# Value products placed among the next unit's scores, and the modulation's steps, PSUM banks and tiles of a fused Fourier/attention layer divided anew

## The chip, the cores and the metric

The kernel runs on one core of a Trainium2 chip. The core has five engines with instruction streams of their own, which meet only through semaphores: TensorE (PE, matmuls into PSUM banks; its weight loads are listed as PEld), VectorE (DVE), ScalarE (ACT), GpSimd (POOL), and SyncE (SP), which here issues nearly all DMA transfers. The metric is the device time of one execution in microseconds, as the median of several runs.

## The reference

One step of a diffusion layer on 1024 latent and 128 context tokens, width 1024, all in fp32. The six modulation vectors come from the conditioning vector and `w_ada`; the first two are needed at the start, the other four only behind the attention. Condensed:

```python
def latent_layer(x, mod, k_ctx, v_ctx, cos, sin, g1, g2, w_in, sink, w_fo, w_ao, w_out, w_ff1, w_ff2):
    sh1, sc1, ga1, sh2, sc2, ga2 = mod          # silu(c) @ w_ada + b_ada, split in six
    h = rmsnorm(x, g1) * (1 + sc1) + sh1
    u_f, q, k, v, g = split_projection(h, w_in) # 512, 1024, 256, 256, 2048 columns
    q, k = apply_rope(q, cos, sin), apply_rope(k, cos, sin)   # 16 heads, 4 key/value heads
    attn_o = latent_attention(q, k, v, k_ctx, v_ctx, sink)    # window of +-128, context keys, sink
    x = x + ga1 * merge_branches(u_f, attn_o, g, w_fo, w_ao, w_out)
    h = rmsnorm(x, g2) * (1 + sc2) + sh2
    return x + ga2 * channel_mixer(h, w_ff1, w_ff2)

def merge_branches(u_f, attn_o, g, w_fo, w_ao, w_out):
    g_f, g_a = split(sigmoid(g))
    m = g_f * (fourier_mix(u_f) @ w_fo) + g_a * (attn_o @ w_ao)   # fourier_mix: real part of a 2-D DFT
    return m @ w_out
```

The context tokens go through the same layer and see only context keys.

## The kernel before

Every fp32 product is made of reduced-precision parts. An operand is split into a high part (a cast, on ScalarE: names in `hi` or `h`) and the rest (a subtraction, on VectorE: names in `lo` or `l`, line 140), and a product is three matmuls, high x high, high x low, low x high (lines 193, 194, 195). Where only one operand is split it is two.

The stages follow each other: normalization and the U projection (to 100 us of the profile), the Fourier mixer in four groups of channels (100 to 176), keys and values and the queries of the first head group (176 to 256), the attention (256 to 716), the Fourier output product `f_unit` (lines 907, 909, 923) around the attention's end (to 740), the merge with `w_ao`, `w_out`, and the two feed-forward products, from about 950 to the end.

**The attention** has 36 units: four groups of four heads, by nine tiles of 128 query tokens. A unit reads 1 to 4 key blocks of 128 (`KWIN`). For each of its heads `score_head` makes the scores in a PSUM bank `s` (lines 752, 753: query by `kth`, `ktl`), VectorE adds the mask and takes the maximum (754), ScalarE takes the exponential (764) and, for each pair of heads, GpSimd divides by the sum (776). `out_t` then transposes a key block of the probabilities into a bank `ptp` (786) and splits it into `ph` (789) and `pl` (140); `out_v` multiplies these with the values into the one bank `o` (801, 802), which behind the last block is copied out by ScalarE (`ot`, 810) and VectorE (`at`, 811). In a round the scores of one unit are followed by the transposes and products of the unit before. The order of TensorE is written out by hand (`manual_schedule`) for the first 34 units; `fill_to` spreads among them single steps of three matmuls of 24-matmul pieces: the queries of the next groups and the gate projections. Other engines' orders are set by the scheduler.

Key blocks are transposed by `put_k` (832), in banks of the same name `ptp`, four blocks at a time, and split into `kth` (834) and `ktl`.

**The modulation** for the later four vectors is 160 small steps (`mod_blocks`): sixteen blocks of ten, eight multiplications and two reductions. A multiplication loads 128 KB into `mraw` (299), multiplies on ScalarE (two instructions, 303; the first of a block into `macc`, the others into the single tile `mprod`) and adds on GpSimd (305). A reduction transposes `macc` into a tile of the name `mraw` too and sums it on VectorE (321, 322); `mod_fold` adds up across partitions on TensorE (268). `mod_step(n)` does the next n steps. Of the 160, 100 are done in the attention, 3 a unit as `MOD_A` says, 20 in the merge stage, where the multiplication is one VectorE instruction (312), and 40 in the feed-forward stage. The Fourier output units use the tile `macc` as their buffer.

Of the kernel before, what the change touches and what calls it, by code (L numbers as in the profile page):

```python
# [18 lines left out]
P = 128  # L19
# [23 lines left out]
KWIN = {0: (0, 3), 1: (0, 4), 2: (1, 4), 3: (3, 4), 4: (4, 4), 5: (6, 4), 6: (7, 4), 7: (8, 3), 8: (11, 1)}  # L43
FILL_F = 2
FILL_0 = 3
MOD_A = (2, 1)
MOD_2 = 2
MOD_B = 60
MOD_LATE = 40
NF = 4  # L50
NF2 = 2
# [5 lines left out]
def backbone_kernel(  # L57
# [185 lines left out]
    MB = 256  # L243

    mview_z = [None, 0]
    MRB = [2, 1]
    split_mul = [True]

    def macc_tile():
# [4 lines left out]
    def mraw_tile():  # L254
        if mview_z[0] is not None:
            mview_z[1] ^= 1
            return mview_z[0][:, 512 + MB * mview_z[1] : 512 + MB + MB * mview_z[1]]
        return zpool[0].tile([P, MB], F32, tag="mraw", name=nm("mraw"), bufs=MRB[0])

    fold = []  # L260

# [24 lines left out]
    def mod_blocks():  # L286
        for blk in range(2 * D // MB, 6 * D // MB):
            st = {}
            for k in range(10):

                def step(blk=blk, k=k, st=st):
                    if k == 5:
                        mod_fold()
                    if k == 0:
                        st["a"] = macc_tile()
                    acc = st["a"]
                    if k < 8:
                        wa = mraw_tile()
                        nc.sync.dma_start(wa, w_ada[k * P : (k + 1) * P, blk * MB : (blk + 1) * MB])
                        if split_mul[0]:  # L300
                            pr_ = acc if k == 0 else zpool[0].tile([P, 2, MB], F32, tag="mprod", name=nm("mprod"), bufs=1)
                            for tok in range(2):
                                nc.scalar.activation(pr_[:, tok, :], wa, AF.Copy, scale=siluc[:, tok, k : k + 1])  # L303
                            if k:
                                nc.gpsimd.tensor_tensor(acc, acc, pr_, ALU.add)  # L305
                            return
                        for tok in range(2):
                            sc_ = siluc[:, tok, k : k + 1]
                            if k == 0:
                                nc.vector.tensor_scalar(acc[:, tok, :], wa, sc_, None, ALU.mult)  # L310
                            else:
                                nc.vector.scalar_tensor_tensor(
                                    acc[:, tok, :], wa, sc_, acc[:, tok, :], ALU.mult, ALU.add
                                )
                        return
                    if k == 8:
                        st["r"] = const.tile([P, 2, MB // 32], F32, tag="red", name=nm("red"), bufs=2)
                    red = st["r"]
                    tok = k - 8
                    tr = mraw_tile()  # L320
                    nc.vector.transpose(tr, acc[:, tok, :])
                    nc.vector.tensor_reduce(
                        red[:, tok, :], tr.rearrange("p (c j) -> p c j", j=32), mybir.AxisListType.X, ALU.add
                    )
                    if k == 9:
                        fold.append((blk, red))

                yield step
# [8 lines left out]
    with ExitStack() as sf:  # L337
# [175 lines left out]
        for gi in range(4):  # L513
# [64 lines left out]
            if e == 1:  # L578
                for i, (lat, o) in enumerate(((bx, 0), (by, 130))):
# [2 lines left out]
                    nc.scalar.copy(f[:, 512:FC], bc[:, o : o + 130])  # L582
                    nc.sync.dma_start(f_d[2 * i + gi // 2], f)
            filler(FILL_F, anchor)

    with ExitStack() as s1x:
        p1 = s1x.enter_context(tc.tile_pool(name="p1", bufs=1))
# [72 lines left out]
        with ExitStack() as skv:  # L660
# [58 lines left out]
            put_kd(kc_, 9)  # L719
            tok_proj_round(ROUNDS[0], OFF_KV, bankk, evac_kv)  # L720
            tok_proj_round(ROUNDS[1], OFF_KV, bankk, evac_kv)
            for piece in q_pieces(0):
                for _ in piece:
                    pass

        pq = s1x.enter_context(tc.tile_pool(name="pq", bufs=1))
        q1 = s1x.enter_context(tc.tile_pool(name="q1", bufs=1, space=PSUM))

# [7 lines left out]
        def score_head(u, h):  # L736
# [10 lines left out]
                u["mx"] = mx  # L747
                nc.gpsimd.tensor_copy(pt[:, :, n : n + 1], nsink[:, h0 : h0 + 2].unsqueeze(2))
            pt, mx = u["pts"][-1], u["mx"]
            sp = q1.tile([P, 512], F32, tag="s", name=nm("s"), bufs=3)  # L750
            qs = qT[:, h, (i % 3) * P : (i % 3 + 1) * P]
            nc.tensor.matmul(sp[:, :n], qs, kth[:, k0 * P : k0 * P + n], start=True, stop=False)
            nc.tensor.matmul(sp[:, :n], qs, ktl[:, k0 * P : k0 * P + n], start=False, stop=True)  # L753
# [27 lines left out]
                    mod_step(min(MOD_A[pr], len(msteps) - MOD_B))  # L781

        def out_t(u, b):
            pst = q1.tile([P, 512], F32, tag="ptp", name=nm("ptp"), bufs=2)
            for h in range(4):
                nc.tensor.transpose(pst[:, h * P : (h + 1) * P], u["pts"][h // 2][:, h % 2, b * P : (b + 1) * P], ident)  # L786
            ph = p1.tile([P, 512], F32R, tag="ph", name=nm("ph"), bufs=3)
            pl = p1.tile([P, 512], F32R, tag="pl", name=nm("pl"), bufs=3)
            nc.scalar.copy(ph, pst)  # L789
            sub(nc.vector, pl, pst, ph)  # L790
            u["p"][b] = ph, pl

        def out_v(u, b):
# [8 lines left out]
            nc.tensor.matmul(po, vst, pl, start=False, stop=(b == nb - 1))  # L802
            if b < nb - 1:
                return
            ot = p1.tile([P, 2, P], F32, tag="ot", name=nm("ot"), bufs=2)
            at = p1.tile([P, 2, P], F32, tag="at", name=nm("at"), bufs=2)
            pv = po.rearrange("p (r e t) -> p e r t", r=2, e=2)
            for e in range(2):
                top, bot = slice(64 * e, 64 * e + 64), slice(64 - 64 * e, 128 - 64 * e)
# [16 lines left out]
            return kd, vg  # L826

        def put_k(kd, q):
            pk = q1.tile([P, 512], F32, tag="ptp", name=nm("ptp"), bufs=2)
            for b in range(4):  # L830
                kb = {"c": 9, "x": 8}.get(KT_ORDER[q * 4 + b], KT_ORDER[q * 4 + b])
                nc.tensor.transpose(pk[:, b * P : (b + 1) * P], kd[:, kb].rearrange("p a d -> p (a d)"), ident)
# [102 lines left out]

        units = [(g, i) for g in range(NG) for i in range(NTT)]
        kv = {0: load_kv(0, kd0)}
        for q in range(3):
            put_k(kv[0][0], q)

# [41 lines left out]

        NMAN = len(units) - 2
        wsum = sum(weight(s) for s in range(NMAN))
        qts = {(0, 0): load_qt(0, 0)}

        def begin(s):
            g, i = units[s]
            if i % 3 == 0 and s + 3 < len(units):
                g1, i1 = units[s + 3]  # L990
                assert g1 in qdone, (s, g1)
                qts[g1, i1 // 3] = load_qt(g1, i1 // 3)
            return {"g": g, "i": i, "q": qts[g, i // 3], "v": kv[g][1], "pts": [], "p": {}}

        def next_keys(g, i):
# [7 lines left out]
                if i == 7:  # L1003
                    put_k(kv[g + 1][0], 1)

        man = ExitStack()
        man.enter_context(tc.manual_schedule(engines={mybir.EngineType.PE}))
        base, pending = 0.0, None
        for s in range(NMAN):
            u = begin(s)  # L1010
            nb = KWIN[pending["i"]][1] if pending else 0
            spots = 4 + (2 * nb + 1 if pending else 0)
            share = NSUB * weight(s) / wsum
            seen = [0]

            def gap():
                seen[0] += 1
                fill_to(base + share * seen[0] / spots)

            for h in range(4):  # L1020
                score_head(u, h)
                gap()
            for b in range(nb):
                out_t(pending, b)
                gap()
                if b:
                    out_v(pending, b - 1)
                gap()
            if nb:
                gap()  # L1030
                out_v(pending, nb - 1)
            base += share
            fill_to(base)
            next_keys(*units[s])
            pending = u
        fill_to(NSUB)
# [3 lines left out]
        for s in range(NMAN, len(units)):  # L1040
            u = begin(s)
            for h in range(4):
                score_head(u, h)
            nb = KWIN[pending["i"]][1]
            for b in range(nb):
                out_t(pending, b)
# [1033 lines left out]
```

## Time and profile before

| | us |
|---|---|
| median of three runs (lowest, highest) | 1684.17 (1682.91, 1687.2) |
| the profiled execution | 1687.13 |
| its span between first and last instruction | 1685.2 |
| TensorE busy | 1624.9 |
| VectorE, ScalarE, GpSimd busy | 1137.1, 897.0, 268.2 |
| mean granted clock of TensorE | 0.993 |

The profile is one execution. A row of a timeline reads: start, duration, engine, line, operation, written tile<-read tiles, shape, count, and in brackets how long the engine had been idle before and what ended that. Where a row stands for several instructions its duration covers them all. Waits are sums of such idle times by the line that waited and the one that ended it. A row of the view by windows gives the stretch, its length, the busy time of PE, PEld, DVE, ACT and POOL with the number of instructions, the granted clock, the DMA engines' share and GB/s. Rows of groups give busy time and mean duration in ns, then the idle time before and what ended it.

### The profile page before, as it was taken

How to read it: one execution, taken by the hardware profiler on the slowest of the kernel's cores; microseconds unless marked ns; L12 is line 12 of the kernel's file. 1: busy time of each engine (PE TensorE's matmuls, PEld its weight loads, DVE VectorE, ACT ScalarE, POOL GpSimd, SP SyncE). 2: the span in 40 equal slices, each digit the busy share in tenths (PEclk: the TensorE clock that was granted, in tenths of full speed). 3: DMA queues.
4: the chain of work that ended last, by engine and by line, in shares of the span. 5: the costliest groups of instructions: out<-in, count | busy, mean ns of one | idle time of the engine just before them, and what ended most of it. 6: DMA issues, size and time to landing. Idle time of an engine off the chain costs nothing.

```text
span 1685.2 us, 24900 instructions
## 1 busy us (share of the span) xinstructions
PE 1624.9 (96%) x8421; PEld 1422.9 (84%) x8421; DVE 1137.1 (67%) x2179; ACT 897.0 (53%) x1743; POOL 268.2 (16%) x368
## 2 busy tenths in 40 slices
PE   6999999999989999999999999999999999999998
PEld 5889888888879889889987788888888888888887
DVE  7663258757657766769657876777776498776764
ACT  7743226767666676655346665444444363444542
POOL 1010014444444444300001500000000200000000
PEclk9999999999999999999999999999999999999999
DMA  8441495435553442389565434445546996666751
GB/s 292 137 148 69 142 218 162 130 111 138 113 123 96 141 114 76 113 267 290 171 206 176 163 113 161 151 158 168 172 143 160 310 389 194 193 194 193 251 162 63
DMA packets 221135, 285.40 MB, mean 169 GB/s; under 512 B 30968, under 2 KB 148664, under 8 KB 220880
## 3 DMA queue, kind: packets, MB, share of 16 engines
q1 hardware_dynamic: 212752, 273.85, 51.6%
q0 software_dynamic: 8256, 9.96, 2.6%
q8 instruction: 66, 1.08, 0.3%
q14 instruction: 61, 0.50, 0.1%
HBM read 205.87 MB, written 77.88 MB: 168 GB/s over the span
## 4 chain that ended last, share of the span: by engine, by line
PE 64%; DVE 9%; DMA 4%; ACT 4%; issue 3%; POOL 2%; SPq 0%; DVEq 0%; ACTq 0%; POOLq 0%
PE x L1806 6%; PE x L1807 6%; PE x L1805 6%; PE x L1409 6%; PE x L1411 6%; PE x L1410 6%; PE mm L193 3%; PE mm L195 3%; PE mm L194 3%; PE ptp L786 2%; DVE pt L754 2%; PE o L802 2%; PE x L194 1%; PE x L195 1%; PE x L193 1%
## 5 line engine op out<-in xcount | busy, mean ns | idle before, releaser
L140 DVE TENSOR_TENSOR wlo<-wraw,whi 128x1024 fp32r<-128x1024 f32 x109 | 138.4, 1272 | 94.7 <-ACT whi L145 94.7
L145 ACT CAST whi<-wraw 128x1024 fp32r<-128x1024 f32 x107 | 111.7, 1049 | 94.6 <-DMA wraw<-in_w_in_dram 18.3
L194 PE MATMUL mm<-BR,whi 128*128 128x384 f32 x408 | 138.5, 339 | 0.0
L1806 PE MATMUL x<-BR 128*128 128x512 f32 (+1 forms) x348 | 132.9, 382 | 0.0
L1807 PE MATMUL x<-BR 128*128 128x512 f32 (+1 forms) x348 | 132.3, 382 | 0.0
L1805 PE MATMUL x<-BR 128*128 128x512 f32 (+1 forms) x348 | 131.4, 382 | 0.0
L193 PE MATMUL mm<-BR,whi 128*128 128x384 f32 x360 | 129.5, 360 | 0.3 <-DVE mods L272 0.3
L140 DVE TENSOR_TENSOR pl<-ptp,ph 128x512 fp32r<-128x512 f32 x124 | 84.7, 687 | 65.2 <-ACT ph L789 64.7
L776 POOL TENSOR_SCALAR pt<-pt,mx 128x512 f32<-128x512 f32 (+2 forms) x144 | 94.7, 670 | 206.3 <-DVE mx L774 204.2
L195 PE MATMUL mm<-BR,wlo 128*128 128x384 f32 x360 | 122.9, 341 | 0.0
L764 ACT ACTIVATE pt<-pt,mx 128x513 f32<-128x513 f32 (+2 forms) x144 | 95.2, 662 | 21.0 <-DVE mx L754 16.5
L1778 ACT CAST BR<-aa 128x512 fp32r<-128x512 f32 x80 | 49.7, 621 | 104.1 <-issue 46.2
L754 DVE CUSTOM_DVE_ANT_0 pt<-s,mask,nsink 128x512 f32<-128x512 f32 (+2 forms) x144 | 94.5, 670 | 14.3 <-PE s L753 11.6
L305 POOL TENSOR_TENSOR macc<-macc,mprod 128x512 f32<-128x512 f32 x70 | 92.4, 1320 | 14.9 <-ACT mprod L303 14.5
L789 ACT CAST ph<-ptp 128x512 fp32r<-128x512 f32 x124 | 70.9, 578 | 41.7 <-PE ptp L786 37.2
L1409 PE MATMUL x<-BR,whi 128*128 128x512 f32 (+2 forms) x204 | 79.6, 390 | 4.1 <-ACT ZR L1433 2.8
L194 PEld LDWEIGHTS mm<-BR,whi 128*128 128x128 f32 x408 | 78.1, 191 | 5.6
L1411 PE MATMUL x<-BR,wlo 128*128 128x512 f32 (+2 forms) x204 | 78.2, 383 | 0.0
L1410 PE MATMUL x<-BR,whi 128*128 128x512 f32 (+2 forms) x204 | 78.0, 382 | 0.0
L193 PE MATMUL mm<-BT,whi 128*128 128x384 f32 x216 | 77.1, 357 | 0.0
L140 DVE TENSOR_TENSOR BR<-aa,BR 128x512 fp32r<-128x512 f32 x80 | 55.2, 690 | 32.4 <-ACT BR L1778 31.5
L786 PE MATMUL ptp<-ident,pt 128*128 128x128 f32 x496 | 75.1, 274 | 1.8 <-POOL pt L776 0.9
(450 smaller groups left out, 4736.3 us busy)
## 6 DMA issues: line engine op xcount, KB each, us to landing
aa<-hr_d SPq DMA_DIRECT2D x108, 256.0 KB
ab<-in_w_ff_dram SPq DMA_DIRECT2D x108, 256.0 KB
hr_d<-ZR SPq DMA_DIRECT2D x104, 256.0 KB
wraw<-in_w_in_dram SPq DMA_DIRECT2D x41, 512.0 KB
wraw<-in_w_ff_dram SPq DMA_DIRECT2D x34, 512.0 KB
mraw<-in_w_ada_dram SPq DMA_DIRECT2D x96, 128.0 KB
wraw<-in_w_out_dram SPq DMA_DIRECT2D x24, 512.0 KB
z_d<-z SPq DMA_DIRECT2D x48, 192.0 KB
```

The lines of the kernel that those rows point to most:

```text
L140: eng.tensor_tensor(dst, raw, hi.bitcast(F32), ALU.subtract)
L145: nc.scalar.copy(hi, raw)
L193: nc.tensor.matmul(out, ah, bh, start=start, stop=False)
L194: nc.tensor.matmul(out, ah, bl, start=False, stop=False)
L195: return nc.tensor.matmul(out, al, bh, start=False, stop=stop).ins
L754: nc.vector.tensor_tensor_reduce(out=pt[:, e, :n], in0=sp[:, :n], in1=mask[:, m0 : m0 + n], scale=-0.125, scalar=nsink[:, h0 + e : h0 + e ...
L1409: nc.tensor.matmul(po, wh, xh, start=(k == 0 and not cont), stop=False, skip_group_check=cont)
L1410: nc.tensor.matmul(po, wh, xl, start=False, stop=False, skip_group_check=cont)
L1411: nc.tensor.matmul(po, wl, xh, start=False, stop=(k == 3), skip_group_check=cont)
L1805: nc.tensor.matmul(ps, xh, bh, start=start, stop=False, skip_group_check=cont)
L1806: nc.tensor.matmul(ps, xh, bl, start=False, stop=False, skip_group_check=cont)
L1807: nc.tensor.matmul(ps, xl, bh, start=False, stop=stop, skip_group_check=cont)
```

## The change

It has six parts.

1. *Value products.* In the hand-written order, product 0 of the unit before follows two fill gaps behind the transposes of block 2 (behind the last where there are fewer than three). Products 1 to 3 are kept in a list and issued one behind each of the next unit's scores. The last two units, which are not ordered by hand, take what is left in the list between their scores.
2. *PSUM banks.* `s` has two banks for three, `ptp` three for two.
3. *Tiles.* `mraw` has three buffers for two, and the transposed result a tile of its own, `mtr`; `ot` and `at` have one buffer for two.
4. *Modulation.* Ten steps behind each of the four Fourier groups, two a unit for three, eight behind the last unit, none in the merge stage, 40 late as before.
5. *First queries and keys.* The six pieces of the first group's queries and the three `put_k` of its keys stand in the hand-written order, one behind the other.
6. *Query loads.* `begin` loads the first tiles too.

```diff
-MOD_A = (2, 1)
+MOD_A = (1, 1)
-MOD_B = 60
+MOD_B = 40
+MOD_F = 10
...
-    MRB = [2, 1]
+    MRB = [3, 1]
...
+    def mtr_tile():
+        if mview_z[0] is not None:
+            return mraw_tile()
+        return zpool[0].tile([P, MB], F32, tag="mtr", name=nm("mtr"), bufs=1)
...
-                    tr = mraw_tile()
+                    tr = mtr_tile()
...
             filler(FILL_F, anchor)
+            mod_step(MOD_F)
...
             tok_proj_round(ROUNDS[1], OFF_KV, bankk, evac_kv)
-            for piece in q_pieces(0):
-                for _ in piece:
-                    pass
...
-            sp = q1.tile([P, 512], F32, tag="s", name=nm("s"), bufs=3)
+            sp = q1.tile([P, 512], F32, tag="s", name=nm("s"), bufs=2)
...
-            pst = q1.tile([P, 512], F32, tag="ptp", name=nm("ptp"), bufs=2)
+            pst = q1.tile([P, 512], F32, tag="ptp", name=nm("ptp"), bufs=3)
...
-            ot = p1.tile([P, 2, P], F32, tag="ot", name=nm("ot"), bufs=2)
-            at = p1.tile([P, 2, P], F32, tag="at", name=nm("at"), bufs=2)
+            ot = p1.tile([P, 2, P], F32, tag="ot", name=nm("ot"), bufs=1)
+            at = p1.tile([P, 2, P], F32, tag="at", name=nm("at"), bufs=1)
...
         kv = {0: load_kv(0, kd0)}
+        man = ExitStack()
+        man.enter_context(tc.manual_schedule(engines={mybir.EngineType.PE}))
+        for piece in q_pieces(0):
+            for _ in piece:
+                pass
         for q in range(3):
             put_k(kv[0][0], q)
...
+        def unit_order(s, u, prev, late):
+            nb = KWIN[prev["i"]][1] if prev else 0
+            out = []
+            for h in range(4):
+                out += [lambda h=h: score_head(u, h), None]
+                if late:
+                    out += [lambda v=late.pop(0): out_v(*v), None]
+            for b in range(nb):
+                out += [lambda b=b: out_t(prev, b), None]
+                if b == 2:
+                    out += [None, lambda: out_v(prev, 0), None]
+            if 0 < nb < 3:
+                out += [None, lambda: out_v(prev, 0), None]
+            late += [(prev, b) for b in range(1, nb)]
+            return out
...
-            for h in range(4):
-                score_head(u, h)
-                gap()
-            for b in range(nb):
-                out_t(pending, b)
-                gap()
-                if b:
-                    out_v(pending, b - 1)
-                gap()
-            if nb:
-                gap()
-                out_v(pending, nb - 1)
+            for f in order:
+                if f is None:
+                    seen += 1
+                    fill_to(base + share * seen / spots)
+                else:
+                    f()
...
             for h in range(4):
                 score_head(u, h)
+                if late:
+                    out_v(*late.pop(0))
```

In the order of the changed kernel lines are numbered three to twelve higher: 752 is 755, 786 is 789, 801 is 804, 810 is 813, 832 is 835, 303 is 309, 911 is 914.

TensorE in the middle of a unit, before: the transposes of block 1 of the unit before (`ptp<-ident,pt`), a filling step, the product of block 0 (`o<-ph`, `o<-pl`), a filling step, the transposes of block 2.

```order
L786 MATMUL ptp_5693<-ident,pt_5441 128x128 x2
L786 MATMUL ptp_5693<-ident,pt_5475 128x128 x2
L193 MATMUL mm_5622<-BT,whi_5344 128x384
L194 MATMUL mm_5622<-BR,whi_5344 128x384
L195 MATMUL mm_5622<-BT,wlo_5345 128x384
L801 MATMUL o_5719<-ph_5680,vg_4058 128x512
L802 MATMUL o_5719<-pl_5681,vg_4058 128x512
L193 MATMUL mm_5722<-BR,whi_5242 128x384
L194 MATMUL mm_5722<-BR,whi_5242 128x384
L195 MATMUL mm_5722<-BR,wlo_5243 128x384
L786 MATMUL ptp_5726<-ident,pt_5441 128x128 x2
L786 MATMUL ptp_5726<-ident,pt_5475 128x128 x2
```

The changed kernel in the middle of a unit, first among the scores: a score, a filling step, the product of block 2 of the unit before (its third into the bank `o_5677`), a filling step, the next score.

```order
L755 MATMUL s_5719<-kth,qT_5133 128x512
L756 MATMUL s_5719<-ktl,qT_5133 128x512
L194 MATMUL mm_5710<-BR,whi_5449 128x384
L195 MATMUL mm_5710<-BR,whi_5449 128x384
L196 MATMUL mm_5710<-BR,wlo_5450 128x384
L804 MATMUL o_5677<-ph_5667,vg_4206 128x512
L805 MATMUL o_5677<-pl_5668,vg_4206 128x512
L194 MATMUL mm_5710<-BR,whi_5449 128x384
L195 MATMUL mm_5710<-BR,whi_5449 128x384
L196 MATMUL mm_5710<-BR,wlo_5450 128x384
L755 MATMUL s_5744<-kth,qT_5133 128x512
L756 MATMUL s_5744<-ktl,qT_5133 128x512
```

And behind the transposes of block 2, where the product of block 0 is the first into a new `o`:

```order
L789 MATMUL ptp_5830<-ident,pt_5541 128x128 x2
L789 MATMUL ptp_5830<-ident,pt_5579 128x128 x2
L194 MATMUL mm_5814<-BR,whi_5360 128x384
L195 MATMUL mm_5814<-BR,whi_5360 128x384
L196 MATMUL mm_5814<-BR,wlo_5361 128x384
L194 MATMUL mm_5814<-BR,whi_5360 128x384
L195 MATMUL mm_5814<-BR,whi_5360 128x384
L196 MATMUL mm_5814<-BR,wlo_5361 128x384
L804 MATMUL o_5845<-ph_5810,vg_4206 128x512
L805 MATMUL o_5845<-pl_5811,vg_4206 128x512
```

Between the transposes of block 1 and the product of block 0 lay one filling step; now the transposes of block 2 and two steps more lie behind it, and the other products stand in the next round.

TensorE where the queries of the first group end, before. The key transposes (`ptp<-ident,kd`) of the first eight blocks stand between two pieces (`mm_2124` and `mm_2163` are two pieces' banks); the scores begin 49 rows later.

```order
L193 MATMUL mm_2124<-BT,whi_2052 128x384
L194 MATMUL mm_2124<-BR,whi_2052 128x384
L195 MATMUL mm_2124<-BT,wlo_2053 128x384
L832 MATMUL ptp_2243<-ident,kd_1621 128x128
L832 MATMUL ptp_2250<-ident,kd_1621 128x128 x4
L193 MATMUL mm_2163<-BR,whi_2017 128x384
L194 MATMUL mm_2163<-BR,whi_2017 128x384
L195 MATMUL mm_2163<-BR,wlo_2018 128x384
```

In the changed kernel: the last piece, all twelve transposes, the first score.

```order
L194 MATMUL mm_2440<-BT,whi_2300 128x384
L195 MATMUL mm_2440<-BT,whi_2300 128x384
L196 MATMUL mm_2440<-BT,wlo_2301 128x384
L835 MATMUL ptp_2479<-ident,kd_1855 128x128 x4
L835 MATMUL ptp_2486<-ident,kd_1855 128x128 x4
L835 MATMUL ptp_2493<-ident,kd_1855 128x128 x4
L755 MATMUL s_2513<-kth,qT_2500 128x384
L756 MATMUL s_2513<-ktl,qT_2500 128x384
```

All three sets now stand between the last query piece and the first score, which reads the first set's `kth` and `ktl`.

ScalarE at the end of the attention, before: copies of the last units (`ot<-o`), the last split (`ph`), and between them the copies of the Fourier output units (`macc<-mm`, `kd<-mm`, `z<-mm`).

```order
L810 COPY ot_7501<-o_7465 64x256
L911 COPY macc_7794<-mm_7779 128x512
L789 CAST ph_7894<-ptp_7889 128x512
L810 COPY ot_7710<-o_7685 64x256
L914 COPY kd_7795<-mm_7780 128x1
L810 COPY ot_7710<-o_7685 64x256
L925 COPY z_7816<-mm_7802 128x130
L911 COPY macc_7863<-mm_7848 128x512
L810 COPY ot_7901<-o_7898 64x256
```

In the changed kernel the copies of the last two units alternate with the multiplications of the last modulation steps (`mprod<-mraw`), and the copy `macc<-mm` of a Fourier output unit follows behind the last of these.

```order
L813 COPY ot_7783<-o_7758 64x256
L309 ACTIVATE mprod_7907<-mraw_7905,siluc 128x256 x2
L813 COPY ot_7783<-o_7758 64x256
L309 ACTIVATE mprod_7921<-mraw_7919,siluc 128x256 x2
L813 COPY ot_8025<-o_8022 64x256
L309 ACTIVATE mprod_7927<-mraw_7925,siluc 128x256 x2
L813 COPY ot_8025<-o_8022 64x256
L309 ACTIVATE mprod_7933<-mraw_7931,siluc 128x256 x2
L146 CAST whi_8139<-wraw_8134 128x1024
L914 COPY macc_7826<-mm_7811 128x512
```

The multiplications are new in this place, and the copies for the Fourier output units moved behind them.

More of the change, by code (lines that the diff above doesn't have):

```diff
@@ L828, in put_k @@
         def put_k(kd, q):
-            pk = q1.tile([P, 512], F32, tag="ptp", name=nm("ptp"), bufs=2)
+            pk = q1.tile([P, 512], F32, tag="ptp", name=nm("ptp"), bufs=3)
             for b in range(4):
@@ L984, in backbone_kernel @@
         wsum = sum(weight(s) for s in range(NMAN))
-        qts = {(0, 0): load_qt(0, 0)}
+        qts = {}
         def begin(s):
             g, i = units[s]
[L989 to L992, printed above, removed]
+            for g1, i1 in units[s : s + 4 : 3] if i % 3 == 0 else ():
+                if (g1, i1 // 3) not in qts:
+                    assert g1 in qdone, (s, g1)
+                    qts[g1, i1 // 3] = load_qt(g1, i1 // 3)
             return {"g": g, "i": i, "q": qts[g, i // 3], "v": kv[g][1], "pts": [], "p": {}}
@@ L1004, in next_keys @@
                     put_k(kv[g + 1][0], 1)
-        man = ExitStack()
-        man.enter_context(tc.manual_schedule(engines={mybir.EngineType.PE}))
-        base, pending = 0.0, None
+        def unit_order(s, u, prev, late):
[13 more added lines that the diff above has]
+            return out
+        base, pending, late = 0.0, None, []
         for s in range(NMAN):
             u = begin(s)
-            nb = KWIN[pending["i"]][1] if pending else 0
-            spots = 4 + (2 * nb + 1 if pending else 0)
+            order = unit_order(s, u, pending, late)
             share = NSUB * weight(s) / wsum
[L1014 to L1018, printed above, removed]
-            for h in range(4):
-                score_head(u, h)
-                gap()
-            for b in range(nb):
-                out_t(pending, b)
-                gap()
-                if b:
-                    out_v(pending, b - 1)
-                gap()
-            if nb:
-                gap()
-                out_v(pending, nb - 1)
+            spots, seen = order.count(None), 0
+            for f in order:
[4 more added lines that the diff above has]
+                    f()
             base += share
-            fill_to(base)
             next_keys(*units[s])
```

## Prediction

> **What bounds the kernel now.** I read the page first, then TensorE's waits for the stretch of the attention, then single waits in the timeline.
>
> ```profile
> PE 1624.9 (96%) x8421; PEld 1422.9 (84%) x8421; DVE 1137.1 (67%) x2179; ACT 897.0 (53%) x1743; POOL 268.2 (16%) x368
> ```
>
> TensorE is busy for 1624.9 of 1685.2 us and the change takes no matmul away, so all that can be won is its idle time, about 60 us, and time at a reduced clock. The waits of TensorE from 250 to 716 us (what was waited for: us, times, longest):
>
> ```profile
> PE o L802 <- DVE pl L140: 8.8, 19, 1.9
> PE o L801 <- ACT ph L789: 8.6, 8, 5.0
> ```
>
> These are value products that wait for their probabilities' high part (`ph`, ScalarE) or low part (`pl`, VectorE): 17.4 us. The largest of them:
>
> ```profile
> 470.80 0.80 PE L801 MATMUL o<-ph,vg 128*128 128x512 f32 x1 [5.01 <-ACT ph L789]
> 466.78 0.91 ACT L303 ACTIVATE macc<-mraw,siluc 128x256 f32<-128x256 f32 x2 [4.74 <-DMA mraw<-in_w_ada_dram]
> 460.02 8.02 SPq L299 DMA_DIRECT2D mraw<-in_w_ada_dram x3
> 563.92 0.51 PE L802 MATMUL o<-pl,vg 128*128 128x512 f32 x1 [1.89 <-DVE pl L140]
> 431.53 0.51 PE L802 MATMUL o<-pl,vg 128*128 128x512 f32 x1 [1.08 <-DVE pl L140]
> ```
>
> The first is a product of block 0; `ph` was late because ScalarE stood for 4.74 us at a modulation step whose load SyncE could not issue (8.02 us in the queue): the transposed result held one of the two `mraw` buffers. The second is of block 2, the third of block 3. Each such wait followed to its block in this way: blocks 1 to 3 have 5.3 us, block 0 has 12.4, of which 5.0 are the one above and 7.4 lie in 13 units, none over 1.2. The first and the last of these:
>
> ```profile
> 270.22 0.49 PE L801 MATMUL o<-ph,vg 128*128 128x512 f32 x1 [0.92 <-ACT ph L789]
> 629.02 0.50 PE L802 MATMUL o<-pl,vg 128*128 128x512 f32 x1 [0.41 <-DVE pl L140]
> ```
>
> Two of these waits also cost clock:
>
> ```profile
> 468.40:476.00 7.60, 5.20 (x16) 4.39 (x17) 2.23 (x5) 3.79 (x10) 2.29 (x4) 0.55 0.26 78
> 564.00:570.00 6.00, 6.00 (x23) 5.48 (x24) 3.51 (x8) 1.55 (x4) 0.00 (x0) 0.72 0.66 210
> 564.43 0.35 PE L194 MATMUL mm<-BR,whi 128*128 128x384 f32 x1
> 564.61 0.50 PE L195 MATMUL mm<-BR,wlo 128*128 128x384 f32 x1
> 564.90 0.52 PE L193 MATMUL mm<-BR,whi 128*128 128x384 f32 x1
> 565.22 0.52 PE L194 MATMUL mm<-BR,whi 128*128 128x384 f32 x1
> ```
>
> The column after POOL is the granted clock, 0.55 and 0.72. Starts of matmuls of 384 columns lie 0.18 us apart before 564.6 and 0.32 after, so a microsecond of work at the low clock loses 0.45. The 5.2 busy us of the first row ran so, and 3.4 us of the second (6 us at a mean of 0.72): 2.3 + 1.5 = 3.8 us.
>
> **The change, part by part.** Blocks 1 to 3 now stand between the next unit's scores. From their transposes to them lie at least 18 more filling matmuls (18 x 0.18 = 3.2 us) with transposes and scores beside; none of their waits was over 1.9 us, so **-5.3**. Block 0 has twelve filling matmuls and two sets of transposes behind its own, where it had twelve and one: 0.4 us more. In the 13 units this leaves 2.9 of 7.4, so **-4.4**. The 5.0 goes if modulation never stalls ScalarE so long: a third `mraw` buffer, an own tile for the transposes, two steps a unit for three; **-5.0**, with **-3.8** of clock. Bounds for the four: -5.3 and -21.2. What comes late next is the single `o` bank: product 0 of a unit must wait for both copies behind the last product of the unit before, which now lies some 5.4 us earlier in TensorE's work. Two score banks for three are no wait by the same working: nine filling matmuls, two products and a score lie between a bank's uses.
>
> The 20 steps of the merge stage go, and with them one wait:
>
> ```profile
> PE mm L268 <- DVE red L322: 1.3, 1, 1.3
> ```
>
> **-1.3**; the 20 steps themselves were VectorE's work beside a busy TensorE.
>
> The start of the attention: the query pieces of group 0 and the key transposes (L832) are now in written order.
>
> ```profile
> 236.51 0.41 PE L832 MATMUL ptp<-ident,kd 128*128 128x128 f32 x2 [2.80 <-ACT rb L708]
> 255.69 1.05 ACT L145 CAST whi<-wraw 128x1024 fp32r<-128x1024 f32 x1 [3.11 <-PE mm L194]
> 256.65 0.58 ACT L834 CAST kth<-ptp 128x512 fp32r<-128x512 f32 x1
> 257.81 1.22 DVE L140 TENSOR_TENSOR wlo<-wraw,whi 128x1024 fp32r<-128x1024 f32 x1
> 258.95 0.55 DVE L636 TENSOR_TENSOR qt<-qt,qt 128x384 f32<-128x384 f32 x1
> 259.42 0.68 DVE L140 TENSOR_TENSOR ktl<-ptp,kth 128x512 fp32r<-128x512 f32 x1
> ```
>
> Before, the transposes of the first four key blocks went between pieces and their casts were done when the scores began. Now they follow the last piece, and right behind them come scores that need `kth` and `ktl`. From the piece's end: weight cast 1.05 on ScalarE, its low part 1.22 on VectorE, L636 0.55 and `ktl` 0.68 make 3.5, with some 0.4 between; TensorE, through with the transposes, has `kth` for the first score at 1.7 and asks for `ktl` at 1.9. **+2.0**, and 0.4 more for `kth` and for the third score's bank, which VectorE frees behind the same queue. The 2.80 wait stays but for 0.45, since the third piece needs rotary steps that VectorE ends then. By the rows a wait of 1.89 brought the low clock, ones of 1.08 and 1.31 did not, so I add one period, **+1.5**. Sum +3.5, bounds -2.8 (the wait of 236.5 gone) and +5.
>
> The Trainium skill ("TensorE: Matmul & The Clock Gate", section "What's actually happening") has the clock halve only after an idle window of about 3.4 us. By that the 2.0 us would cost no clock and this term be 1.5 less; the 1.89 us wait above, with its low clock from 564.6 on, speaks against it.
>
> The U projection and the Fourier stage take 40 steps: 32 multiplications with an addition each, and eight reductions.
>
> ```profile
> 83.26 3.04 ACT L344 COPY u<-x 128x512 f32<-128x512 f32 x6 [3.46 <-PE x L233]
> 81.46 0.34 SPq L664 DMA_DIRECT2D rope<-in_rope_dram  x1
> L303 ACT ACTIVATE mprod<-mraw,siluc 128x256 f32<-128x256 f32 x138 | 62.9, 503 | 20.9 <-POOL macc L305 20.3 <-DMA mraw<-in_w_ada_dram 0.5
> L305 POOL TENSOR_TENSOR macc<-macc,mprod 128x512 f32<-128x512 f32 x70 | 92.4, 1320 | 14.9 <-ACT mprod L303 14.5
> 100.00:126.00 26.00, 25.31 (x146) 24.31 (x145) 19.67 (x28) 12.16 (x20) 6.86 (x7) 1.00 0.51 155
> 126.00:150.00 24.00, 24.00 (x143) 22.39 (x142) 8.21 (x24) 8.53 (x17) 1.49 (x2) 1.00 0.23 84
> 143.07 0.59 ACT L581 COPY f<-x 128x512 f32<-128x512 f32 x1 [3.50 <-PE x L195]
> ```
>
> ScalarE's first step stands ahead of the six copies that free U's banks, and its load can be issued only when the tiles of the stage before go, at 81.5: about **+1.5** for TensorE (0 to 3). From there to 176 us the 32 steps are 32 x (2 x 0.50 + 1.32) = 74 us of a chain over ScalarE and GpSimd, in 93 us where ScalarE is a third busy and waits 2 to 3.5 us for TensorE in each group. So most hides there; for copies that stand behind a step that waits for its addition I take **+3** (0 to 12).
>
> The end of the attention: eight steps stand behind the last unit's. Before, there were none.
>
> ```profile
> 707.94 1.74 POOL L776 TENSOR_SCALAR pt<-pt,mx 128x128 f32<-128x128 f32 x2 [1.90 <-DVE mx L774]
> 711.78 0.63 PE L786 MATMUL ptp<-ident,pt 128*128 128x128 f32 x4 [0.86 <-DVE pl L140]
> 718.82 0.74 PE L907 MATMUL mm<-BR,whi 128*128 128x512 f32 x2 [0.44 <-ACT z L925]
> 721.40 0.50 PE L801 MATMUL o<-ph,vg 128*128 128x512 f32 x1 [0.91 <-DVE at L811]
> 726.56 0.70 PE L907 MATMUL x<-BR,whi 128*128 128x512 f32 x2 [1.11 <-DVE at L811]
> ```
>
> From GpSimd's last normalization (709.7) to the first product in the next stage's banks (726.6) TensorE waited 3.3 us. In the new order of ScalarE the six last multiplications alternate with the copies of the last two units (L810), and each waits for the addition before it, as `mprod` is one buffer. The copy that frees the last bank stands behind the fifth: 1.3 + 4 x 2.3 + 1.0 + 0.7 = 12.2 us after the normalization. `macc` is needed by the Fourier output units too, so these can't fill in until the chain is through; TensorE has about 3 us of work. Idle 9.2 for 3.3: **+6**, a clock period **+1.5**, and **+1** as the merge's loads start nearer to their use. Sum +8.5, bounds 0 (the chain is done before) and +14 (loads late by 5).
>
> **Sum**: -5.3 - 4.4 - 5.0 - 3.8 - 1.3 = -19.8, and 3.5 + 1.5 + 3 + 8.5 = +16.5: -3.3 us. The profiled execution took 1687.1 around its span of 1685.2; the median of the three runs is 1684.2. The same difference from the median gives **1681**.
>
> **Rivals.** *The added work hides* (28%): the chain at the end finds its steps done early because GpSimd is idle for most of the tail, and the Fourier stage swallows its steps; then only the 3.5 and 1.5 are left, with 1 us for the rest: -13.8, 1670. For it: the idle times of ScalarE above. Against it: one `mprod` buffer, 20.3 us of waiting for the addition in the row above.
>
> *GpSimd's additions hold VectorE up in the Fourier stage* (17%), slower:
>
> ```profile
> 101.40 1.79 DVE L518 TENSOR_TENSOR st<-u 128x512 f32<-128x512 f32 x1
> 109.27 0.69 DVE L518 TENSOR_TENSOR st<-u 128x512 f32<-128x512 f32 x1
> 101.33 1.31 POOL L519 TENSOR_TENSOR e<-u 128x512 f32<-128x512 f32 x1 [75.94 <-ACT u L344]
> ```
>
> One instruction took 1.79 us beside a GpSimd addition and 0.69 without. The page of the Trainium skill "GPSIMD Engine Reference", section "1. Specifications", has GpSimd share VectorE's interface to the memory, with contention for instructions of two inputs there; the trace agrees by these rows. Four such instructions a group, 1.1 late each, are 4.4 against some 3 us of slack: 1.4 x 4 groups; with one held-up ScalarE copy of 1.3 a group and 1 us at the first, 12 us for my 3: 1690. It decides from where additions lie beside the group's preparation rather than its products. Against it: VectorE is a third busy from 126 on.
>
> *Block 0 doesn't gain* (13%): its small waits stay at 7.4, for the copies of `o` now lie just ahead: +4.4, 1685.5.
>
> **How the numbers follow.** The forecast has 42%. Of it about 9 points lie below 1679.1, the rest within 0.3% (5 us, about what a measurement of this kernel can tell from no change). Faster: 27 points of the first rival and these 9, 0.36. Slower: 14 of the second, 5 of the third and 3 of the forecast, 0.22. Within: 0.42. The forecast's own range is 1675 to 1689; for 8 in 10 it reaches to both outer rivals and past them by a part of their bounds, 1667 to 1695.
>
> **What would show it.** Right: the waits of `o` for `ph` and `pl` fall from 17.4 to about 3 us and the clock stays full from 260 to 690; a wait of about 2 us at the first score for `ktl`; one of about 9 us at the first product in the `x` banks for `at` near the end of the attention; in the Fourier stage single waits for `pqh` or `sth` of 1 us. Wrong: no wait at the end of the attention (first rival), or additions beside lengthened VectorE instructions and over 8 us of waits before 176 (second).

## The result and the profile after

The changed kernel takes **1695.51 us** (median of 4 runs, 1692.07 to 1696.1) against 1683.54 us (4 runs, 1682.18 to 1687.2): a ratio of 1.0063, with a 95% interval of 1.0042 to 1.0085. It is slower, where 1681 and no clear difference had been forecast, and lies just above the range of 1667 to 1695. The profiled execution took 1695.82 us for 1687.13, its span is 1694.0 us for 1685.2. That is 8.8 us where the medians are 12.0 apart: the profiled execution of the kernel before is near the slowest of its runs. In the changed kernel's rows the lines of the shared helpers are numbered one higher than before (140 is 141, 193 to 195 are 194 to 196).

First TensorE's waits of the changed kernel in the stretch of the units, 260 to 690 us (what was waited for: us, times, longest):

```profile
PE s L756 <- DVE ktl L141: 5.0, 1, 5.0
PE o L804 <- DVE at L814: 2.9, 1, 2.9
PE o L805 <- DVE pl L141: 1.6, 5, 0.8
PE o L804 <- ACT ph L792: 1.2, 2, 0.8
```

The waits for `ph` and `pl` fell from 17.4 to 2.8 us, as forecast; what had not been there is the wait for `ktl` (forecast as 2) and the one for the copies out of `o`. Then 690 to 760 us, where the attention ends:

```profile
PE o L804 <- DVE at L814: 7.6, 2, 4.1
PE x L910 <- DVE at L814: 3.8, 1, 3.8
PE x L194 <- ACT ER L1128: 3.1, 1, 3.1
PE x L910 <- ACT fy L914: 1.6, 1, 1.6
PE mm L910 <- DVE mods L278: 1.2, 1, 1.2
PE x L912 <- ACT fo L917: 1.0, 1, 1.0
```

and the same stretch by windows (length, busy PE, PEld, DVE, ACT, POOL, granted clock, DMA share, GB/s), the changed kernel first, then the kernel before from the same place in its work:

```profile
690.00:760.00 70.00, 51.04 (x233) 42.68 (x233) 35.65 (x70) 29.76 (x71) 15.48 (x17) 0.78 0.53 166
706.00:776.00 70.00, 65.66 (x377) 60.22 (x376) 51.02 (x98) 38.78 (x81) 4.82 (x9) 1.00 0.81 253
```

In 70 us TensorE idles 19 us for 4, and the clock is 0.78 for 1.00. The rest is read from four marks, before and after: the first product of U, the last product of the Fourier stage, the first score, and the first product of the stage behind the merge.

```profile
35.71 0.40 PE L231 MATMUL x<-whi,BR 128*128 128x512 f32 x1
172.72 0.28 PE L575 MATMUL x<-pxl,dhi 128*128 128x130 f32 x1
256.03 0.42 PE L752 MATMUL s<-kth,qT 128*128 128x384 f32 x1
843.43 0.48 PE L1240 MATMUL x<-whi,BR 128*128 128x512 f32 x1
```

```profile
33.55 0.40 PE L232 MATMUL x<-whi,BR 128*128 128x512 f32 x1
178.73 0.28 PE L581 MATMUL x<-pxl,dhi 128*128 128x130 f32 x1
260.08 0.44 PE L755 MATMUL s<-kth,qT 128*128 128x384 f32 x1
851.95 0.39 PE L1251 MATMUL x<-whi,BR 128*128 128x512 f32 x1
```

The first product of U starts 2.16 us earlier, which the change doesn't account for: over the profiles of all runs it starts between 33.2 and 36.1 with no order in it. From there to the last Fourier product 137.0 us became 145.2, **+8.2**. From that to the first score it is 2.0 us less: the wait of 2.80 us at 236.5 with its low clock is gone, one of 1.9 us at 241.7 with full clock has come. From the first score to behind the merge 587.4 became 591.9, **+4.5**, where -19.8 of gains and +3.9 and +8.5 of costs had been forecast. From there to the end the two differ by 0.3 us.

### The profile page after: what moved, and what is told of

Same layout as the page of the kernel before. It is cut to its first block, busy times and chain, and to the rows that moved or that the text cites. A ratio compares the mean times of both kernels' runs of the same rounds, so it can differ in the third digit from the quotient of the medians.

```text
span 1694.0 us, 24957 instructions
## 1 busy us (share of the span) xinstructions
PE 1624.9 (96%) x8421; PEld 1430.3 (84%) x8421; DVE 1134.8 (67%) x2147; ACT 912.3 (54%) x1775; POOL 290.4 (17%) x382
## 3 DMA queue, kind: packets, MB, share of 16 engines
q8 instruction: 66, 1.08, 0.3%
## 4 chain that ended last, share of the span: by engine, by line
PE 49%; DVE 2%; issue 2%; ACT 1%; DMA 1%; POOL 0%; SPq 0%; POOLq 0%; ACTq 0%; DVEq 0%
PE x L1817 6%; PE x L1816 6%; PE x L1818 6%; PE x L1420 6%; PE x L1422 6%; PE x L1421 6%; PE x L196 2%; PE x L194 2%; PE x L195 2%; PE mm L1467 1%; PE mm L1466 1%; PE mm L1465 1%; PE mm L1817 1%; PE mm L1816 1%; PE mm L1818 1%
## 5 line engine op out<-in xcount | busy, mean ns | idle before, releaser
L311 POOL TENSOR_TENSOR macc<-macc,mprod 128x512 f32<-128x512 f32 x84 | 113.5, 1352 | 108.3 <-ACT mprod L309 97.3
L309 ACT ACTIVATE mprod<-mraw,siluc 128x256 f32<-128x256 f32 x168 | 76.8, 505 | 32.1 <-POOL macc L311 31.8
```

## The experiments

Each was timed beside the kernel before on the same chip, in at least four runs.

**e1**, no steps behind the last unit.

```diff
-MOD_B = 40
+MOD_B = 50
```

> The changed kernel with MOD_B 50: no modulation step behind the last unit, ten in the merge stage again. Theory (the chain of eight steps at the end costs about 11 us of waits for at and some 9 us of low clock up to 756 us): 12 to 20 us less than the changed kernel, 1676 to 1683, and the three waits of 4.10, 3.52 and 3.82 us gone. Rival (TensorE has run ahead and waits there in any case, for one bank o and single ot and at): the waits stay over 8 us in sum, 1690 to 1696.

1669.29 us; 0.9910 of before (0.9892 to 0.9927). That is 26 us less than the changed kernel, more than the theory asked for. The stretch of 690 to 760 us in this kernel:

```profile
690.00:760.00 70.00, 66.71 (x384) 62.17 (x383) 53.92 (x107) 39.48 (x84) 3.83 (x8) 1.00 0.86 272
```

15.7 us less idle, and the full clock. From the first score to behind the merge it takes 566.0 us, 25.9 less than the changed kernel, so nearly the whole difference is here. One wait of 2.3 us for `at` is left, which is the part of the rival that holds.

**e2**, modulation as before.

```diff
-MOD_A = (1, 1)
-MOD_B = 40
-MOD_F = 10
+MOD_A = (2, 1)
+MOD_B = 60
+MOD_F = 0
```

> The changed kernel with all modulation where it was before (none in the Fourier stage, 3 a unit, 20 in the merge stage), products, banks, tiles and keys as changed. Theory: the gain of e1 and the 7 to 8 us that TensorE lost before 178 us: 1666 to 1675, below the kernel before by 9 to 17. Rival (the deferred products and the banks themselves cost the time, modulation only moves it): 1685 to 1692.

1664.82 us; 0.9886 (0.9867 to 0.9905): a little more gain than the theory had, and far from the rival. It is 4.5 us less than e1. In the traces the steps in the U and Fourier stages cost more than that: from the first product of U to the last Fourier product this kernel takes 136.7 us (the kernel before 137.0), e1 143.0. Part comes back up to the first score, which counted from the U products is 0.3 us earlier than before here and 3.7 later in e1.

**e3**, the Fourier steps alone.

```diff
-MOD_A = (2, 1)
-MOD_B = 60
+MOD_A = (1, 1)
+MOD_B = 50
+MOD_F = 10
...
             filler(FILL_F, anchor)
+            mod_step(MOD_F)
```

> The kernel before with ten modulation steps behind each Fourier group and two a unit (1, 1), ten in the merge stage; nothing else changed. Theory (the Fourier steps hold ScalarE's copies): TensorE arrives 6 to 8 us later at the keys, and at most 5 us come back in the attention: 1684 to 1691. Rival (the steps hide, and the delay before 178 us comes from the third mraw buffer and the new allocation): no more than 2 us later at the keys, 1677 to 1684.

1690.33 us; 1.0036 (1.0021 to 1.0051). In the profiled execution, with 1694.9 us the slowest of six, the first score is 7.6 us late when counted from the U products, and next to nothing comes back in the attention, although a unit has a third less modulation: as the theory had it.

**e4**, key transposes between the pieces.

```diff
-        for piece in q_pieces(0):
+        for n, piece in enumerate(q_pieces(0)):
             for _ in piece:
                 pass
-        for q in range(3):
-            put_k(kv[0][0], q)
+            if 2 < n:
+                put_k(kv[0][0], n - 3)
```

> The changed kernel with the three sets of key transposes behind query pieces 4, 5 and 6 instead of all behind the last. Theory (at the start of the attention TensorE waits for ktl of the first set because it is made last, 5.05 us and 2.5 us of low clock): only the third set is late, which the first unit doesn't read, 5 to 8 us less than the changed kernel, 1687 to 1691. Rival (VectorE's rotary steps of the last piece are in front of ktl wherever the transposes stand): 0 to 2 us, 1693 to 1696.

1692.53 us, 3 less than the changed kernel: between the two. The wait for `ktl` is gone, and another stands in its place, a piece that waits 3.3 us for VectorE's rotary steps to free its bank (the other of the two, of about 2 us, is there in the changed kernel too):

```profile
PE mm L194 <- DVE qt L638: 5.5, 2, 3.3
```

**e5**, the deferral alone: `unit_order` and the list `late` put into the kernel before.

```diff
+        def unit_order(s, u, prev, late):
...
-                out_t(pending, b)
-                gap()
-                if b:
-                    out_v(pending, b - 1)
...
+            order = unit_order(s, u, pending, late)
```

> The kernel before with the deferred value products alone; banks (three s, two ptp), tiles, modulation and keys as before. Theory (the deferral itself brings the 20.7 us that e2 was ahead from the first score to the merge's end, and the banks and tiles only make room): 1660 to 1668. Rival (without a third mraw buffer the 5 us stall of ScalarE stays, without a third ptp bank transposes wait for the low parts): half of the gain at most, 1670 to 1678.

1700.13 us; 1.0102 (1.0081 to 1.0123). Neither range: with two `ptp` banks the deferral alone makes the kernel slower by 1%. The wait that the rival named is there, and larger than it said. TensorE's waits from 250 to 716 us:

```profile
PE ptp L786 <- DVE pl L140: 28.2, 27, 4.1
...
PE o L802 <- DVE pl L140: 1.3, 2, 1.0
...
PE o L801 <- ACT ph L789: 0.7, 2, 0.4
```

and in one unit the transposes of the first three key blocks:

```profile
306.54 0.60 PE L786 MATMUL ptp<-ident,pt 128*128 128x128 f32 x4
307.50 0.60 PE L786 MATMUL ptp<-ident,pt 128*128 128x128 f32 x4
310.73 0.66 PE L786 MATMUL ptp<-ident,pt 128*128 128x128 f32 x4 [2.10 <-DVE pl L140]
```

The products don't wait any more. But they had kept the transposes apart: without them three sets come within 2 us, the third into the bank of the first, which is free only when its `pl` is made. The old wait has gone from the products to the transposes and has grown.

**e6**, no additions in the Fourier steps.

```diff
-                            if k:
+                            if k and blk >= 2 * D // MB + 4:
                                 nc.gpsimd.tensor_tensor(acc, acc, pr_, ALU.add)
```

> e1's kernel without GpSimd's additions in the four blocks that the Fourier stage takes; these blocks' modulation then lacks seven of its eight products, ScalarE's multiplications and their loads stay. Theory (additions beside VectorE's two-input instructions, and multiplications that wait for them, cost the time before 178 us): 3 to 6 us less than e1's 1669.3, 1663 to 1666, and L524 on VectorE back from 1448 ns to below 1000. Rival (the multiplications and the loads in SyncE's queue cost it): 1668 to 1671.

1669.35 us, e1's time, with a modulation that is incomplete in these blocks: the theory falls. What it says of VectorE holds, though. One line of the Fourier preparation, in e1 and here, from 83 to 176 us:

```profile
L524 DVE TENSOR_TENSOR st<-u 128x512 f32<-128x512 f32 x4 | 5.8, 1447 | 0.0
```

```profile
L524 DVE TENSOR_TENSOR st<-u 128x512 f32<-128x512 f32 x4 | 2.7, 687 | 0.6 <-ACT u L350 0.5
```

Without the additions it takes half as long (the Trainium skill, "GPSIMD Engine Reference", section "1. Specifications", has the two engines contend for instructions with two SBUF inputs; the rows agree), and no time is won: TensorE waits for ScalarE's `pqh`, 3.3 us at the longest in e1 and 3.1 here. Whether the multiplications on ScalarE or their loads hold `pqh` up is left open: this kernel has both. The scheduler also ordered the engines anew in it, so only the sum is compared.

**e7**, e2 with queries and keys of the first group ordered by the scheduler.

```diff
+            for piece in q_pieces(0):
+                for _ in piece:
+                    pass
...
-        man = ExitStack()
-        man.enter_context(tc.manual_schedule(engines={mybir.EngineType.PE}))
-        for piece in q_pieces(0):
-            for _ in piece:
-                pass
```

> e2's kernel with queries and key transposes of the first group ordered by the scheduler as before. Theory (the written order costs the wait of 3.7 us for ktl and a low clock period of 1.5): 1659 to 1662. Rival (the scheduler's order has its own 2.8 us wait and period at 236 us, so nothing is won): 1664 to 1666.

**1660.10 us**; 0.9858 (0.9842 to 0.9873), the fastest of all: the kernel before with deferral, banks and tiles. It takes 561.8 us from the first score to behind the merge, 25.6 less than before:

```profile
253.58 0.34 PE L759 MATMUL s<-kth,qT 128*128 128x384 f32 x1
815.39 0.47 PE L1252 MATMUL x<-whi,BR 128*128 128x512 f32 x1
```

**e8**, no additions in the last block.

```diff
-                            if k:
+                            if k and (blk != 2 * D // MB + 11 or k < 2):
                                 nc.gpsimd.tensor_tensor(acc, acc, pr_, ALU.add)
```

> The changed kernel without GpSimd's additions in the block of the last eight steps, whose modulation then lacks six products; ScalarE's multiplications stay, but mprod is free at once and macc after the first. Theory (the chain of multiplication and addition over one mprod buffer, which holds the copies of o and, through macc, the Fourier output units): most of e1's 26 us come back, 1671 to 1678. Rival (the 5.5 us of ScalarE's multiplications between the copies are enough): 1686 to 1694.

1673.36 us, 22 of e1's 26 us, with a modulation that lacks these additions. That leaves some 4 us for ScalarE's multiplications between the copies. The output units go back among the last products in this kernel, since `macc` is free.

**e9**, e5 with two score banks and three transpose banks.

```diff
-            sp = q1.tile([P, 512], F32, tag="s", name=nm("s"), bufs=3)
+            sp = q1.tile([P, 512], F32, tag="s", name=nm("s"), bufs=2)
...
-            pst = q1.tile([P, 512], F32, tag="ptp", name=nm("ptp"), bufs=2)
+            pst = q1.tile([P, 512], F32, tag="ptp", name=nm("ptp"), bufs=3)
```

> e5's kernel (before, with the deferral) with two s and three ptp banks; tiles, modulation and keys as before. Theory (the 28.2 us that e5's transposes waited for the low parts are the missing third ptp bank, and the tiles add only the 5 us stall of ScalarE at a modulation load): 1660 to 1668. Rival (the third mraw buffer and the own transpose tile carry a good part of the gain): 1670 to 1680.

1671.24 us; 0.9929 (0.9906 to 0.9952). The third bank turns a loss of 17 us into a gain of 12 (by the two ratios, of 1684 us); the wait of the transposes falls from 28.2 to 0.8. The time lies in the rival's range, 11 us above e7: with two `mraw` buffers and the shared transpose tile there are waits for `o`'s copies of 5.2 us here (0.4 in e7), and at the start of the attention, where the scheduler put the pieces otherwise, one of 3.7 us with low clock. How much of the 11 is that start wasn't separated, and the tiles weren't taken one by one.

**e10**, an own buffer for the output units.

```diff
-    MRB = [3, 1]
+    MRB = [2, 1]
...
-                    tr = mtr_tile()
+                    tr = mraw_tile()
...
-            y = p1.tile([P, 2, MB], F32, tag="macc", name=nm("macc"), bufs=1)
+            y = p1.tile([P, 2, MB], F32, tag="fyb", name=nm("fyb"), bufs=1)
```

> The changed kernel with a buffer of its own for the Fourier output units instead of macc (paid for by mraw with two buffers and the transposes in them). Theory (of e1's 26 us about half is TensorE waiting for the copies of o behind multiplications, half comes from the output units that can't fill in while macc is held): 1678 to 1686, waits for at at the end still over 4 us. Rival (the copies alone hold everything): 1690 to 1697.

1686.43 us; 1.0010 (0.9995 to 1.0025), just above the theory's range: 9 us less than the changed kernel although `mraw` has a buffer less. The waits for `at` at the end fall from 11.4 to 5.0 us.

**e11**, two `mprod` buffers, `mraw` and transposes as in e10.

```diff
-tag="mprod", name=nm("mprod"), bufs=1
+tag="mprod", name=nm("mprod"), bufs=2
```

> The changed kernel with two mprod buffers (paid for in the same way). Theory (each round at the end is 0.9 us of multiplication and 1.3 of addition one behind the other; with two buffers the additions alone pace it): the chain of six is 5 to 6 us shorter, 1686 to 1691. Rival (GpSimd's additions pace it already): 1693 to 1697.

1694.45 us, the rival's time. Its mechanism isn't what the trace shows: the multiplications run ahead, wait for their loads now (0.7 and 0.2 us), and the copies still come late, one of them behind VectorE's two sums for a weight tile (1.08 and 1.75 us). As `mraw` lost a buffer here, the second `mprod` alone wasn't tested.

**e12**, e7 with all early steps in the units.

```diff
-MOD_A = (2, 1)
-MOD_B = 60
+MOD_A = (2, 2)
+MOD_B = 40
```

> e7's kernel with four modulation steps a unit instead of three, so that all 120 early steps are done by the 30th unit, none in the merge stage and none behind the last unit. Theory (steps cost time where TensorE has no other work, and a unit has room for a fourth): the 1.3 us wait for the merge stage's reduction goes and little is lost, 1656 to 1660. Rival (ScalarE's copies of block 0 and of o become late again at four steps): 1661 to 1668.

1669.47 us; 0.9914 (0.9895 to 0.9934), 9 slower than e7 and past the rival's range. The copies of `o` are late again, 6.3 us for 0.4, which speaks against room for a fourth step. At the start of the attention the scheduler put the pieces otherwise, with a wait of 3.4 us and low clock; its share wasn't separated.

## Why the prediction was wrong

**The step that failed is the end of the attention.** The place and the chain of multiplications, additions and copies were right; the term was put at +8.5 us with an upper bound of +14, and e1 measures it at 26. Three things were too small. (That the single `mprod` paces the chain is not confirmed: e11 gave it two buffers and won nothing, though at the price of one `mraw` buffer.) GpSimd's chain in the changed kernel, from the last normalization on:

```profile
692.96 0.72 POOL L779 TENSOR_SCALAR pt<-pt,mx 128x128 f32<-128x128 f32 x2 [1.50 <-DVE mx L777]
693.64 1.28 POOL L311 TENSOR_TENSOR macc<-macc,mprod 128x512 f32<-128x512 f32 x1
696.49 1.26 POOL L311 TENSOR_TENSOR macc<-macc,mprod 128x512 f32<-128x512 f32 x1 [1.57 <-ACT mprod L309]
698.96 1.09 POOL L881 MEMSET wraw<- 1x512 f32 x2 [1.21 <-DVE wraw L879]
700.10 1.08 POOL L872 MEMSET wraw<- 1x512 f32 x2
701.26 2.26 POOL L311 TENSOR_TENSOR macc<-macc,mprod 128x512 f32<-128x512 f32 x1
```

- *The chain.* It was reckoned as additions and multiplications alone. GpSimd also clears the weight tiles of the output units in it, and these wait for VectorE and for loads. So 3.5 us lie between the second and the third addition, where between later ones it is 1.08, and the third takes 2.26 us for 1.3: the first product in the `x` banks came at 710.5, 16.8 us after the normalization, not 12.2.
- *What follows it.* TensorE's wait was forecast at 9.2 us in one place; it was 11.4 in three. Behind it the output units, pushed into the next stage's time one after the other by `macc`, waited again (`fy`, `fo`, `mods`), and the merge's first casts, which wait for loads, held TensorE for 3.1 us where +1 was forecast: 19 us of idle time in all for 4. e10 frees `macc` and gets 9 us back; e8 takes the additions away and gets 22.
- *The clock.* One period of 3.4 us at half clock was counted. The profile has four stretches between 701 and 756 us, of 13.65, 6.83, 6.83 and 3.41 us, with some 21 us of work in them. At the prediction's 0.45 a microsecond that is about 9 us. Three of them (the fourth, from 728.64, is shown in the last section):

```profile
701.34:714.99 13.65, 6.31 (x15) 4.09 (x14) 6.47 (x11) 6.40 (x14) 8.65 (x7) 0.50 0.39 112
738.88:745.71 6.83, 5.78 (x13) 4.03 (x14) 2.38 (x5) 1.80 (x5) 0.00 (x0) 0.50 0.89 272
752.53:755.94 3.41, 3.41 (x13) 3.41 (x12) 3.41 (x8) 2.33 (x7) 0.00 (x0) 0.50 0.98 319
```

**Blocks 1 to 3 and block 0** were right, and the gain was larger than said: e7, where the merge's wait is gone too, has 25.6 us for the 19.8 of the four terms and that wait. (Counted along TensorE's order the 17.4 us are 5.2 in blocks 1 to 3 and 12.2 in block 0, of which 7.2 lie in 12 units; the prediction's 5.3, 12.4, 7.4 and 13 add up to a little too much.) The excess may lie in the way waits are counted. In the kernel before:

```profile
628.22 0.40 PE L801 MATMUL o<-ph,vg 128*128 128x512 f32 x1
629.02 0.50 PE L802 MATMUL o<-pl,vg 128*128 128x512 f32 x1 [0.41 <-DVE pl L140]
629.36 0.34 PE L193 MATMUL mm<-BT,whi 128*128 128x384 f32 x1
```

A wait is counted from the modelled end of the matmul before it. Unhindered, these start 0.23 us apart; here 0.80 and then 0.34, a loss of 0.68 for a listed 0.41. For 27 listed waits that makes some 7 us more than 17.4. That it accounts for the whole excess is argued, not shown.

**The banks** were a gap in the working: what the third `ptp` bank is worth was not asked, only what two score banks cost (nothing, rightly: the changed kernel has no wait for them in the units). e5 and e9 show that without the third bank there is no gain but a loss of 17 us. For the copies of `o` no wait was forecast; in the changed kernel there is one of 2.9 us, in a unit where VectorE stood 3.8 us at a rotary step that waited for a transfer.

**The start of the attention** (+3.5 forecast) was right in its place and too small: 5.05 us for `ktl` and a low clock over 5.7 us of work, 2.5 us. VectorE made six rotary steps and two low parts of weights ahead of it; the prediction had counted one of each. Against the scheduler's own order the part costs 4.7 us (e2 to e7), and e4 shows that moving the transposes alone moves the wait.

**U and Fourier** (+1.5 and +3) were too small as well: 8.2 us in the changed kernel, within the bounds of the two terms. Between e1 and e2, which differ in the place of the steps, it is 6.3. The largest part is one wait, where single ones of 1 us had been forecast, and the clock behind it:

```profile
PE x L194 <- ACT pqh L555: 3.5, 1, 3.5
127.90:134.73 6.83, 6.24 (x21) 5.16 (x21) 4.62 (x13) 2.34 (x6) 3.83 (x3) 0.50 0.21 67
```

The clock was half for 6.83 us. In kernels with the same steps there the cost varies with that stretch: 6.0 us with 3.41 us of low clock in e1, 10.3 with 10.24 in e10. So the place was as forecast, and the multiplications and their loads are the causes that are left. The second rival's is not among them: GpSimd's additions do hold VectorE up, and without them no time is won (e6).

**The merge's wait** of 1.3 us went as forecast.

Of the rivals none came true: the slow side was reached through the forecast's own term at the end of the attention. That the sum came out only 0.5 us above the range is luck: the gains were 5.8 us larger than said, and hid a part of the 17 us that the end cost beyond its term. Put together from the runs, first score to behind the merge: -25.6 for deferral, banks and tiles (e7), +4.9 for the written order of the first keys (e2 less e7), -0.7 for fewer steps in the units and ten in the merge (e1 less e2), +25.9 for the eight steps at the end: +4.5. These four are the steps of one path from the kernel before to the changed one, so their sum has to be what the changed kernel shows; each step alone is the difference of two profiled executions.

## What to carry to other kernels

Work that is hidden in a loop has to be finished before the loop ends: behind the last iteration the same steps form a chain that nothing covers, and everything in the order behind them waits (26 us for six multiplications with their additions, of some 2.3 each, and two reductions). When a consumer is moved later, what it kept apart moves together, and its producer needs the buffers for it: the deferral alone cost 17 us, with the third transpose bank it gained 12. And the cost of a stall is to be counted with its followers: the idle time listed, what start-to-start times show beyond it, the clock, and what could have filled it but shared a buffer.

## What the hardware showed that I had not expected

The low clock came after much less than a long wait. The changed kernel's row from 725.2 to 728.6, and the next:

```profile
725.20:728.64 3.44, 2.80 (x23) 2.58 (x22) 2.00 (x3) 1.27 (x3) 0.00 (x0) 1.00 0.19 76
728.64:735.47 6.83, 5.68 (x14) 4.46 (x14) 2.13 (x13) 0.58 (x1) 0.00 (x0) 0.50 0.45 125
```

TensorE was busy for 2.80 of 3.44 us (the last 0.6 with four matmuls of 16 columns), with no wait over 0.64, and ran the next 6.8 us at half; a wait of 1.9 us at 241.7 us in the same kernel brought no low clock:

```profile
241.00:246.00 5.00, 4.30 (x25) 4.31 (x26) 3.53 (x8) 2.07 (x5) 1.72 (x3) 1.00 0.98 333
```

Nor did one of 3.05 us in e6, with TensorE busy for 0.55 of 3.60 us:

```profile
125.00:128.60 3.60, 0.55 (x4) 0.23 (x2) 3.35 (x7) 3.57 (x10) 0.29 (x1) 1.00 0.65 211
128.60:136.00 7.40, 7.40 (x42) 6.40 (x43) 1.82 (x10) 4.90 (x12) 1.42 (x1) 1.00 0.43 139
```

So the length of one wait doesn't decide. The Trainium skill ("TensorE: Matmul & The Clock Gate", section "What's actually happening") names an idle window of about 3.4 us as the condition and lets the windows run freely; the lengths of 13.65, 6.83 and 3.41 us, whole multiples of 3.41, agree with such windows; the condition of idleness does not, at 2.80 us of work in one. What decides stays open.
